# Down-projection of a ConvFFN: one accumulating transfer per result, and six of eight output pairs finished in SBUF

## The chip, the cores and the metric

The kernel runs on one core of one Trainium2 chip. The metric is the device time of one execution in microseconds. Times are the median of several executions; the profile shows one execution.

## What is computed

One inference step of a hybrid layer over T = 592 tokens (16 meta tokens, 512 of a prompt, 8 x 8 samples) with D_MODEL = 2048 and D_FF = 6144, all in float32. Cut to the part that matters:

```python
x = x + jnp.einsum("bte,ed->btd", y_mix, w_o)
xn2 = rmsnorm(x, g_ffn)
up = jnp.einsum("btd,df->btf", xn2, w_up)
gate, val = jnp.split(up, [D_FF], axis=-1)
gate_c, new_fconv = causal_dwconv(gate, st_fconv, conv_f_w)
hid = jax.nn.gelu(gate_c + conv_f_b) * val
x = x + jnp.einsum("btf,fd->btd", hid, w_down)      # the down-projection
...
y = rmsnorm(x, g_final)
```

## The kernel before

Everything is held with features on the 128 partitions and tokens along the free dimension. A float32 factor is split into a high and a low part (`hi`, `lo`; ScalarE copies the rounded high part, VectorE subtracts), and a product takes three matmuls: high by high, high by low, low by high.

**The up- and down-projection use a Strassen-like scheme.** Weights come in pairs of blocks, two by two; tokens are cut into two halves of H2 = 288 columns. Seven products of combined blocks replace eight. `prep` (lines 251 to 284) loads 8 blocks of weights (`raw`, three buffers, issued on SP), forms the combinations on VectorE (one operation of 512 columns, two of 256) and splits seven blocks of each of two units into `wh` and `wl` (four buffers of each). The inputs' combinations are built by `forms` into slots `h0`/`l0` to `h7`/`l7` of the pool `slots`, and one more set in other buffers (`v`, `o`, `st`, `fb`): nine slots for 22 input pairs, so input k lies in slot k mod 9.

**The down-projection runs in three passes** (`s` = 0, 1, 2) over the 22 input pairs k, since only nine are in SBUF at a time. In each pass there is one job ("d", s, p) for each of the eight output pairs p. A job's units are the k from `CUT[p][s]` to `CUT[p][s+1]`: pass 0 takes 4, 5, 6, 7, 8, 8, 9, 9 units for p = 0 to 7, pass 1 takes 9 each, pass 2 takes 9, 8, 7, 6, 5, 5, 4, 4. One unit is 7 products of 3 matmuls with 288 columns. Two units make a group; with an odd number of units a group holds the last unit of one job and the first of the next.

A job's products collect in four PSUM tiles: `s6` (product P6, a single bank), `dq` (P2, Q3), `dp` (P1, R7) and `dr` (P5, R4). There are two buffers for the first kind and three for the others, so the next job's matmuls wait until each is read. When a job ends, `done_d` (lines 471 to 490) turns them into two SBUF tiles of four blocks, `e23` and `e17`, by five ScalarE copies and two VectorE additions, and adds them into two DRAM accumulators per output pair, `xa[p]` (which holds the residual at first) and `xb[p]`, by two transfers on POOL's queue with `accum_op=AD`. `urgent()` raises the priority of these reads.

**The tail** multiplies the last four blocks of `hid` (input pairs 22 and 23, `kh`/`kl`, made by `last_hidden`) without the scheme: for two ranges of tokens (304 and 272 columns) and 16 output blocks f, 12 matmuls each (line 712). `done_t` adds the PSUM result to `xp[f // 2]`, squares it and sums the squares for the final norm. `load_xp` (lines 537 to 541) fetches `xp[p]` from DRAM, first `xa[p]`, then `xb[p]` added onto it. Before the change `xp` of pairs 0 to 2 is asked for when job ("d", 2, 5) ends, the others when all jobs have ended. The tail's weights, eight groups of 8 blocks, are split into `th` and `tl`; they lie in slots 4, 5, 0 and 1 (`TAILW`).

**Order.** The instructions of each engine run in an order that a planner fixes when the kernel is built, from priorities and the durations that it assumes. It may put an instruction ahead of its place in the program: transfers of `kf`, which the code asks for when job ("d", 2, 3) ends, stand in the profile at 2446.80 us, in job ("d", 2, 0). SP issues the loads of weights, POOL all transfers of `sb`, `xa`, `xb`, `xp` and `kf`.

Tiles by name: `raw` weights as loaded, `wh`/`wl` split weights, `fh`/`fl` split inputs, `e` the tiles of `done_d`, `sgl`/`dbl` PSUM, `th`/`tl` split tail weights. Lines 210 and 216 are the helpers through which nearly all VectorE additions and ScalarE copies go, line 552 the matmuls of both projections, line 247 the loads of weights, lines 486, 488 and 490 the accumulations, 540 and 541 the loads of `xp`.

Of the kernel before, what the change touches and what calls it, by code (L numbers as in the profile page):

```python
# [7 lines left out]
F32 = mybir.dt.float32  # L8
F32R = mybir.dt.float32r
AF = mybir.ActivationFunctionType  # L10
ALU = mybir.AluOpType

P = 128
# [4 lines left out]
KD = 16  # L18
NA, NB, NF = 12, 8, 48
# [7 lines left out]
NTF = T - T1  # L27
# [30 lines left out]
NSL = 9  # L58
NWB = 4
NRAW = 3  # L60
TAILW = (4, 5, 0, 1)
NPL = 4
NTL = 4
H1, H2 = NTM // 2, NTF // 2
# [135 lines left out]
def ffn(ctx, tc, xstack, one, dram, x1, rstd, ones, epst, warm, cv, wf, sfc, out, fst):  # L200
# [4 lines left out]
    nc = tc.nc  # L205
    V, A, G = nc.vector, nc.scalar, nc.gpsimd
    M, AD, SU = ALU.mult, ALU.add, ALU.subtract

    def tt(o, a, b, op, e=None):
        return (e or V).tensor_tensor(out=o, in0=a, in1=b, op=op)  # L210
# [4 lines left out]
    def act(o, a, f, **k):  # L215
        A.activation(out=o, in_=a, func=f, **k)  # L216
# [7 lines left out]
    urgent = lambda: tc.high_priority(offset=URGENT)  # L224
# [26 lines left out]
    def prep():  # L251
        q, u = divmod(state["spl"], 2)
        while state["raw"] < min(q + NRAW, len(FG)):
            load()
        t = raws.pop(q) if u else raws[q]
        kind, i, _ = FG[q]
        if kind == "s":
            r = t.rearrange("p (s c) f -> p s (c f)", s=8)
            if u == 0:
                tt(r[:, 4:6], r[:, 2:4], r[:, 0:1].to_broadcast([P, 2, 2 * P]), AD)  # L260
                tt(r[:, 6], r[:, 5], r[:, 2], AD)
                tt(r[:, 7], r[:, 6], r[:, 1], AD)
            src, n = r[:, 1:8, u * P:u * P + P], 7
        else:
            src, n = t[:, 4 * u:4 * u + 4], 4
        if kind == "t":
            if u == 0:
                g = i // 2
                tag = TAILW[g // 2]
                if g % 2 == 0:  # L270
                    for c in "hl":
                        tail[c] = sl.tile([P, 16, P], F32R, tag=f"{c}{tag}", name="t" + c)
                tail[g] = [tail[c][:, 8 * (g % 2):8 * (g % 2) + 8] for c in "hl"]
                hi, lo = tail[g]
                act(hi, t[:, 0:8], AF.Copy)
                tt(lo, t[:, 0:8], hi.bitcast(F32), SU)
            spls[q, u] = None
        else:
            hi = w_p.tile([P, n, P], F32R, tag="wh", name="wh")
            lo = w_p.tile([P, n, P], F32R, tag="wl", name="wl")  # L280
            act(hi, src, AF.Copy)
            tt(lo, src, hi.bitcast(F32), SU)
            spls[q, u] = hi, lo
        state["spl"] += 1
# [10 lines left out]

    xd = [dram.tile([P, 2, NTM], F32, name=f"xd{p}") for p in range(KD // 2)]
    xa = [dram.tile([P, 4, H2], F32, name=f"xa{p}") for p in range(KD // 2)]
    xb = [dram.tile([P, 4, H2], F32, name=f"xb{p}") for p in range(KD // 2)]
    hd = [dram.tile([P, 2, NTF], F32, name=f"hd{m}") for m in range(NF // 2)]
    qa = xq_p.tile([P, 2, NTM], F32, tag="sb", name="qa")  # L300
    qb = xq_p.tile([P, 2, NTM], F32, tag="xt", name="qb")
# [169 lines left out]
    def done_d(s, p, ps):  # L471

        s6, dq, dp, dr = ps
        e6 = rp.tile([P, H2], F32, tag="e6", name="e6")
        e23 = rp.tile([P, 4, H2], F32, tag="e23", name="e23")
        e17 = rp.tile([P, 4, H2], F32, tag="e17", name="e17")
        w = lambda d: d[:, :, 0:H2]
        with urgent():
            act(e6, s6[:, 0:H2], AF.Copy)
            act(e23[:, 0:4:3], w(dq), AF.Copy)  # L480
            act(e23[:, 1], dq[:, 1, 0:H2], AF.Copy, scale=-1.0)
            act(e23[:, 2], dq[:, 0, 0:H2], AF.Copy, scale=-1.0)
            tt(e17[:, 1:3], w(dp), e6.unsqueeze(1).to_broadcast([P, 2, H2]), AD)
            act(e17[:, 0:4:3], w(dp), AF.Copy)
            tt(e17[:, 1:3], w(dr), e17[:, 1:3], AD)
        nc.gpsimd.dma_start(out=xa[p], in_=e23, accum_op=AD)
        if s:
            nc.gpsimd.dma_start(out=xb[p], in_=e17, accum_op=AD)
        else:
            nc.gpsimd.dma_start(out=xb[p], in_=e17)  # L490

    kh, kl = [], []

    def last_hidden():
        ts = []
        for c in range(NTL // 2):
            ts.append(xq_p.tile([P, 2, NTF], F32, tag=("sb", "xt")[c], name="kf"))
            nc.gpsimd.dma_start(out=ts[c], in_=hd[NF // 2 - NTL // 2 + c])
        for c, t in enumerate(ts):
            h = sl.tile([P, 2, NTF], F32R, tag=f"h{6 + c}", name="kh")  # L500
            l = sl.tile([P, 2, NTF], F32R, tag=f"l{6 + c}", name="kl")
            act(h, t, AF.Copy)
            tt(l, t, h.bitcast(F32), SU)
            for j in range(2):
                kh.append(h[:, 1 - j])
                kl.append(l[:, 1 - j])
# [30 lines left out]
    def load_xp(p, pl_, tag):  # L537
        xp[p] = pl_.tile([P, 2, NTF], F32, tag=tag, name="xp")
        w = xp[p].rearrange("p f (h m) -> p (f h) m", h=2)
        nc.gpsimd.dma_start(out=w, in_=xa[p])  # L540
        nc.gpsimd.dma_start(out=w, in_=xb[p], accum_op=AD)

    def products(u, hi, lo, names, ps, H):
        nonlocal mm
# [14 lines left out]
    while FG[q][0] != "t":  # L559
        kind, i, _ = FG[q]  # L560
        halves = weights(q)
        if kind == "p":
            r, k0 = i
            if k0 == 0:
                d = psd()
                ps = [(d[:, 0, 0:H1], d[:, 1, 0:H1])]
                if r == 0:
                    d = psd()
                    ps.append((d[:, 0, 0:H1], d[:, 1, 0:H1]))
                else:  # L570
                    ps.append((pss()[:, 0:H1], pss()[:, 0:H1]))
            for k in range(k0, k0 + 4):
                hi, lo = halves[(k - k0) // 2]
                for j in range(2):
                    o = (k - k0) % 2 * 2 + j
                    rh, rl = ph[k // 2][:, k % 2], pl[k // 2][:, k % 2]
                    for n, (l, x) in enumerate(((hi, rh), (hi, rl), (lo, rh))):
                        for h, (c0, w) in enumerate(HPL):
                            mm = nc.tensor.matmul(ps[j][h], l[:, o], x[:, c0:c0 + w],  # L579
                                                  start=k == 0 and n == 0,  # L580
                                                  stop=k == KD - 1 and n == 2)
            if r == 0 and k0 == 4:
                norm(mm)
            if k0 + 4 == KD:
                (plain_v if r else plain_f)(0, ps)
            if r:
                for kp in (k0 // 2, k0 // 2 + 1):
                    build_x(kp)
        else:
            same = i[0][0] == i[1][0]  # L590
            H = H2 if i[0][0][0] == "d" else H1
            for us in ([i] if same else [[i[0]], [i[1]]]):
                job = us[0][0]
                if job not in pst:
                    pst[job] = (pss(), psd(), psd(), psd())
                    if job == lastc:
                        for k in (0, 1):
                            load_h(k)
                hold = left[job]
                for n in NAMES:  # L600
                    left[job] = hold
                    for u in us:
                        products(u, *halves[i.index(u)], n, pst[job], H)
                        left[job] -= 1
                if left[job] == 0:
                    {"f": done_f, "v": done_v, "d": done_d}[job[0]](*job[1:], pst.pop(job))
                    if job == lastc:
                        nc.gpsimd.dma_start(out=fst.rearrange("p (n c) -> p n c", c=18), in_=fa)
                for u in us:
                    for k in due.get(nunit, ()):  # L610
                        build_h(k)
                    nunit += 1
                if job == ("d", 2, 3) and left[job] == 0:
                    last_hidden()
                if job == ("d", 2, 5) and left[job] == 0:
                    for p, tag in enumerate(("o", "fb", "v")):
                        load_xp(p, rp, tag)
        q += 1

    for p, tag in ((3, "h2"), (4, "l2"), (5, "h3"), (6, "l3")):  # L620
        load_xp(p, sl, tag)

    load_xp(7, rp, "e23")
    sq_a = xq_p.tile([P, 3, 304], F32, tag="sb", name="sq_a")
    sq_b = xq_p.tile([P, 3, 304], F32, tag="xt", name="sq_b")
    sq_c = rp.tile([P, 2, 304], F32, tag="st", name="sq_c")
    rz2 = rp.tile([P, 2, 304], F32, tag="e17", name="rz2")
    SZ = [(sq_a[:, 0], sq_b[:, 0]), (sq_c[:, 0], sq_c[:, 1])]
    SQ = [sq_a[:, 1], sq_b[:, 1], sq_a[:, 2], sq_b[:, 2]]
    later = []  # L630

    def defer(n, fn):
# [624 lines left out]
```

## Time and profile before

| | us |
|---|---|
| median of 3 runs | 2675.44 |
| lowest, highest | 2668.48, 4513.52 |
| profiled execution, its own time | 2674.38 |
| its span in the profile | 2672.6 |
| mean granted clock of TensorE | 0.986 |

| Stretch of the span | us |
|---|---|
| mixer and up-projection | 0 to 2058 |
| down-projection, passes 0 and 1 | 2058 to 2435 |
| pass 2 | 2435 to 2593 |
| tail, first range of tokens | 2593 to 2628 |
| tail, second range | 2628 to 2658 |
| final norm of the second range and its output | 2658 to 2673 |

PE is TensorE's matmuls, PEld its loads of weights, DVE VectorE, ACT ScalarE, POOL GpSimd, SP the engine that issues the loads of weights. In a row of waits, "X <- Y: a, n, m" says that X waited for Y for a us in total, n times, m us at the longest. In a row of the timeline the bracket holds the engine's idle time before the instruction and what ended it. In a group of instructions the numbers behind the bar are busy us and mean ns of one, then idle us before them.

### The profile page before, as it was taken

What the parts mean: (1) busy time and instruction counts of PE and PEld (TensorE: products, weight loads), DVE (VectorE), ACT (ScalarE), POOL (GpSimd) and SP (SyncE); (2) the same over time, 40 slices, a digit from 0 to 9 for tenths busy, and PEclk for the clock granted to TensorE, in tenths of its full rate; (3) what the DMA queues carried; (4) which work ended last, traced back from release to release, by engine and by line L of the source; (5) the groups of instructions that cost most, each with busy time, mean ns of one, the idle gap of its engine ahead of it and who ended that gap; (6) DMA issues with size and microseconds to landing.
All of it is one profiled execution on the core that took longest, in us unless ns stands there. A gap on an engine that the chain in (4) does not pass through costs nothing.

```text
span 2672.6 us, 46445 instructions
## 1 busy us (share of the span) xinstructions
PE 2581.6 (97%) x18974; PEld 2562.4 (96%) x18974; DVE 1960.0 (73%) x2699; ACT 1188.9 (44%) x1760; POOL 503.4 (19%) x636
## 2 busy tenths in 40 slices
PE   8999999999999978999999999999999999999986
PEld 8999999999999977999999999999999999999986
DVE  8663556536636579888888888888889978778655
ACT  6542434334325354454444454545445545435442
POOL 3341323314224530000000000000000100001023
PEclk9999999999999988999999999999999999999989
DMA  5222222222222433333333333333334756656695
GB/s 167 80 88 79 80 80 83 82 82 80 80 80 90 179 128 117 122 104 113 104 106 106 112 103 114 104 114 104 114 104 126 205 147 187 156 145 170 154 233 143
DMA packets 90518, 318.32 MB, mean 119 GB/s; under 512 B 10816, under 2 KB 15424, under 8 KB 90304
## 3 DMA queue, kind: packets, MB, share of 16 engines
q1 hardware_dynamic: 68720, 233.47, 27.9%
q0 software_dynamic: 21152, 81.43, 11.6%
q8 instruction: 148, 2.42, 0.4%
q14 instruction: 66, 0.54, 0.1%
q10 hardware_dynamic: 432, 0.46, 0.1%
HBM read 257.91 MB, written 57.39 MB: 118 GB/s over the span
## 4 chain that ended last, share of the span: by engine, by line
PE 53%; DVE 5%; DMA 4%; issue 1%; ACT 1%; POOL 0%; DVEq 0%; ACTq 0%; POOLq 0%
PE dbl L552 44%; PE sgl L552 7%; DMA raw<-wf 2%; DVE wl L210 2%; PE dbl L579 1%; DMA sb<-hd 1%; DVE fl L210 1%; DMA xp<-xa 1%; DVE raw L210 1%; DVE xt L210 1%; DVE xp L213 1%; DVE sb L213 0%; DMA xp<-xb 0%; PE dbl L712 0%; ACT e L216 0%
## 5 line engine op out<-in xcount | busy, mean ns | idle before, releaser
L552 PE MATMUL dbl<-fh,wh 128*128 128x290 f32 (+1 forms) x3264 | 969.6, 297 | 14.7 <-ACT e L216 10.9
L552 PE MATMUL dbl<-fl,wh 128*128 128x290 f32 (+1 forms) x3264 | 966.8, 296 | 2.2 <-DVE fl L210 2.2
L552 PE MATMUL dbl<-fh,wl 128*128 128x290 f32 (+1 forms) x3264 | 966.4, 296 | 2.1 <-DVE wl L210 2.0
L216 ACT ACTIVATE wh<-raw 128x896 fp32r<-128x896 f32 (+1 forms) x560 | 498.6, 935 | 600.3 <-issue 356.5
L210 DVE TENSOR_TENSOR wl<-raw,wh 128x896 fp32r<-128x896 f32 (+1 forms) x560 | 583.7, 1074 | 106.8 <-ACT wh L216 103.7
L552 PEld LDWEIGHTS dbl<-fh,wh 128*128 128x128 f32 x3264 | 617.7, 189 | 18.8 <-ACT e L216 13.8
L552 PEld LDWEIGHTS dbl<-fl,wh 128*128 128x128 f32 x3264 | 618.5, 190 | 3.3 <-DVE fl L210 3.3
L552 PEld LDWEIGHTS dbl<-fh,wl 128*128 128x128 f32 x3264 | 618.3, 190 | 3.0 <-DVE wl L210 3.0
L210 DVE TENSOR_TENSOR raw<-raw 128x256 f32<-128x256 f32 (+1 forms) x816 | 412.4, 510 | 151.1 <-DMA raw<-wf 141.1
L787 ACT ACTIVATE wh<-raw 128x512 fp32r<-128x512 f32 x277 | 172.5, 628 | 395.6 <-PE ps L1168 343.3
L1168 PE MATMUL ps<-xh,wl 128*128 128x290 f32 (+4 forms) x1536 | 335.6, 299 | 3.7 <-DVE wl L775 3.7
L1168 PE MATMUL ps<-xh,wh 128*128 128x290 f32 (+4 forms) x1536 | 331.3, 297 | 2.9 <-ACT wh L787 2.9
L1168 PE MATMUL ps<-xl,wh 128*128 128x290 f32 (+4 forms) x1536 | 333.8, 299 | 0.0
L775 DVE TENSOR_TENSOR wl<-raw,wh 128x512 fp32r<-128x512 f32 x192 | 152.9, 802 | 193.0 <-ACT wh L787 192.6
L1168 PEld LDWEIGHTS ps<-xh,wl 128*128 128x128 f32 x1536 | 256.8, 190 | 4.2 <-DVE wl L775 4.2
L1168 PEld LDWEIGHTS ps<-xh,wh 128*128 128x128 f32 x1536 | 256.7, 190 | 3.8 <-ACT wh L787 3.1
L1168 PEld LDWEIGHTS ps<-xl,wh 128*128 128x128 f32 x1536 | 254.9, 189 | 0.0
L775 POOL TENSOR_TENSOR wl<-raw,wh 128x512 fp32r<-128x512 f32 x86 | 117.9, 1371 | 312.5 <-ACT wh L787 302.5
L552 PE MATMUL sgl<-fh,wl 128*128 128x290 f32 (+1 forms) x544 | 164.8, 303 | 10.0 <-DVE wl L210 9.9
L552 PE MATMUL sgl<-fh,wh 128*128 128x290 f32 (+1 forms) x544 | 162.3, 298 | 3.3 <-ACT wh L216 2.5
L552 PE MATMUL sgl<-fl,wh 128*128 128x290 f32 (+1 forms) x544 | 162.2, 298 | 2.6 <-DVE fl L210 2.6
L1168 PE MATMUL ps<-kh,wl 128*128 128x290 f32 x640 | 138.5, 297 | 0.0
(222 smaller groups left out, 3219.5 us busy)
## 6 DMA issues: line engine op xcount, KB each, us to landing
raw<-wf SPq DMA_DIRECT2D x288, 512.0 KB, 3.6
raw<-w SPq DMA_DIRECT2D x135, 512.0 KB, 3.6
hd<-v POOLq DMA_DIRECT2D x48, 288.0 KB, 2.8
xa<-e POOLq DMA_DIRECT2D x24, 576.0 KB, 7.4
xb<-e POOLq DMA_DIRECT2D x24, 576.0 KB, 7.1
sb<-hd POOLq DMA_DIRECT2D x22, 576.0 KB, 4.4
x<-x SPq DMA_DIRECT2D x16, 296.0 KB, 5.3
xd<-x POOLq DMA_DIRECT2D x16, 290.0 KB, 2.6
```

Of the source, the lines that this page charges most:

```text
L210: return (e or V).tensor_tensor(out=o, in0=a, in1=b, op=op)
L213: V.scalar_tensor_tensor(out=o, in0=a, scalar=s, in1=b, op0=op0, op1=op1)
L216: A.activation(out=o, in_=a, func=f, **k)
L552: mm = nc.tensor.matmul(o, l[a], r[z], start=left[job] == total[job] and n == 0, stop=left[job] == 1 and n == 2)
L579: mm = nc.tensor.matmul(ps[j][h], l[:, o], x[:, c0:c0 + w], start=k == 0 and n == 0, stop=k == KD - 1 and n == 2)
L775: return (e or V).tensor_tensor(out=o, in0=a, in1=b, op=op)
L787: A.activation(out=o, in_=a, func=f, **k)
L1168: mm = nc.tensor.matmul(ps[:, b, 0:n], l, r[:, c0:c0 + n], start=(first and m == 0), stop=(last and m == 2))
```

## The change

`done_d` is rewritten. In passes 0 and 1, and for output pairs 0 and 1 of pass 2, it forms all four blocks in one tile `e` (buffers `e17` and `e23` in turn) with four ScalarE copies and four VectorE additions, and adds that tile into `xa[p]` by one accumulating transfer; `xb` is gone. For output pairs 2 to 7 of pass 2 it adds the PSUM tiles to `xp[p]` in SBUF, by seven VectorE operations, with no ScalarE copy and no transfer.

For that `xp[p]` of pairs 2 to 7 is loaded during pass 2 into slots 4, 5 and 6, when jobs 0, 1 and 2 end; pairs 0 and 1 are loaded into `e17` and `e23` when job 3 ends. Each load is one transfer. `kf`, the input of `last_hidden`, is loaded when job 0 ends, and split when job 5 ends, into other buffers. The tail's weights move: group 0 to the buffers of `kf`, groups 1 to 6 to slots 1, 2 and 3, group 7 to `l7`. The squares of the final norm move to slot 0.

```diff
         if kind == "t":
             if u == 0:
                 g = i // 2
-                tag = TAILW[g // 2]
-                if g % 2 == 0:
-                    for c in "hl":
-                        tail[c] = sl.tile([P, 16, P], F32R, tag=f"{c}{tag}", name="t" + c)
-                tail[g] = [tail[c][:, 8 * (g % 2):8 * (g % 2) + 8] for c in "hl"]
+                if g == 0:
+                    tail[g] = [xq_p.tile([P, 8, P], F32R, tag=c, name="t" + c) for c in ("sb", "xt")]
+                elif g == 7:
+                    t7 = sl.tile([P, 16, P], F32R, tag="l7", name="t7")
+                    tail[g] = [t7[:, 0:8], t7[:, 8:16]]
+                else:
+                    j, o = divmod(g + 1, 2)
+                    if o == 0:
+                        tail["h"], tail["l"] = (sl.tile([P, 16, P], F32R, tag=f"{c}{j}", name="t" + c)
+                                                for c in "hl")
+                    tail[g] = [tail[c][:, 8 * o:8 * o + 8] for c in "hl"]
...
     def done_d(s, p, ps):
 
         s6, dq, dp, dr = ps
-        e6 = rp.tile([P, H2], F32, tag="e6", name="e6")
-        e23 = rp.tile([P, 4, H2], F32, tag="e23", name="e23")
-        e17 = rp.tile([P, 4, H2], F32, tag="e17", name="e17")
         w = lambda d: d[:, :, 0:H2]
+        if s < 2 or p < 2:
+            e6 = rp.tile([P, H2], F32, tag="e6", name="e6")
+            e = rp.tile([P, 4, H2], F32, tag=("e17", "e23")[p % 2], name="e")
+            on, off = e[:, 0:4:3], e[:, 1:3]
+            with urgent():
+                act(e6, s6[:, 0:H2], AF.Copy)
+                act(on, w(dq), AF.Copy)
+                act(e[:, 1], dq[:, 1, 0:H2], AF.Copy, scale=-1.0)
+                act(e[:, 2], dq[:, 0, 0:H2], AF.Copy, scale=-1.0)
+                tt(off, w(dp), off, AD)
+                tt(on, w(dp), on, AD)
+                tt(off, w(dr), off, AD)
+                tt(off, off, e6.unsqueeze(1).to_broadcast([P, 2, H2]), AD)
+            nc.gpsimd.dma_start(out=xa[p], in_=e, accum_op=AD)
+            return
+        t = xp[p].rearrange("p f (h m) -> p (f h) m", h=2)
+        on, off = t[:, 0:4:3], t[:, 1:3]
         with urgent():
-            act(e6, s6[:, 0:H2], AF.Copy)
-            act(e23[:, 0:4:3], w(dq), AF.Copy)
-            act(e23[:, 1], dq[:, 1, 0:H2], AF.Copy, scale=-1.0)
-            act(e23[:, 2], dq[:, 0, 0:H2], AF.Copy, scale=-1.0)
-            tt(e17[:, 1:3], w(dp), e6.unsqueeze(1).to_broadcast([P, 2, H2]), AD)
-            act(e17[:, 0:4:3], w(dp), AF.Copy)
-            tt(e17[:, 1:3], w(dr), e17[:, 1:3], AD)
-        nc.gpsimd.dma_start(out=xa[p], in_=e23, accum_op=AD)
-        if s:
-            nc.gpsimd.dma_start(out=xb[p], in_=e17, accum_op=AD)
-        else:
-            nc.gpsimd.dma_start(out=xb[p], in_=e17)
+            tt(off, s6[:, 0:H2].unsqueeze(1).to_broadcast([P, 2, H2]), off, AD)
+            tt(on, w(dq), on, AD)
+            tt(t[:, 1], t[:, 1], dq[:, 1, 0:H2], SU)
+            tt(t[:, 2], t[:, 2], dq[:, 0, 0:H2], SU)
+            tt(on, w(dp), on, AD)
+            tt(off, w(dp), off, AD)
+            tt(off, w(dr), off, AD)
...
+    def load_last():
+        for c in range(NTL // 2):
+            kfs.append(xq_p.tile([P, 2, NTF], F32, tag=("sb", "xt")[c], name="kf"))
+            nc.gpsimd.dma_start(out=kfs[c], in_=hd[NF // 2 - NTL // 2 + c])
+
     def last_hidden():
...
-            h = sl.tile([P, 2, NTF], F32R, tag=f"h{6 + c}", name="kh")
-            l = sl.tile([P, 2, NTF], F32R, tag=f"l{6 + c}", name="kl")
+            h = (sl, rp)[c].tile([P, 2, NTF], F32R, tag=("h7", "fb")[c], name="kh")
+            l = rp.tile([P, 2, NTF], F32R, tag=("o", "v")[c], name="kl")
...
         nc.gpsimd.dma_start(out=w, in_=xa[p])
-        nc.gpsimd.dma_start(out=w, in_=xb[p], accum_op=AD)
...
-                if job == ("d", 2, 3) and left[job] == 0:
-                    last_hidden()
-                if job == ("d", 2, 5) and left[job] == 0:
-                    for p, tag in enumerate(("o", "fb", "v")):
-                        load_xp(p, rp, tag)
+                if job[0] == "d" and job[1] == 2 and left[job] == 0:
+                    n = job[2]
+                    if n == 0:
+                        load_last()
+                    for p, tag in {0: ((2, "h4"), (3, "l4")), 1: ((4, "h5"), (5, "l5")),
+                                   2: ((6, "h6"), (7, "l6"))}.get(n, ()):
+                        load_xp(p, sl, tag)
+                    if n == 3:
+                        for p, tag in ((0, "e17"), (1, "e23")):
+                            load_xp(p, rp, tag)
+                    if n == 5:
+                        last_hidden()
...
-    for p, tag in ((3, "h2"), (4, "l2"), (5, "h3"), (6, "l3")):
-        load_xp(p, sl, tag)
-
-    load_xp(7, rp, "e23")
-    sq_a = xq_p.tile([P, 3, 304], F32, tag="sb", name="sq_a")
-    sq_b = xq_p.tile([P, 3, 304], F32, tag="xt", name="sq_b")
...
+    sq_a = sl.tile([P, 6, 304], F32, tag="h0", name="sq_a")
+    sq_b = sl.tile([P, 4, 304], F32, tag="l0", name="sq_b")
...
```

More of the change, by code (lines that the diff above doesn't have):

```diff
@@ L60 @@
 NRAW = 3
-TAILW = (4, 5, 0, 1)
 NPL = 4
@@ L297, in ffn @@
     xa = [dram.tile([P, 4, H2], F32, name=f"xa{p}") for p in range(KD // 2)]
-    xb = [dram.tile([P, 4, H2], F32, name=f"xb{p}") for p in range(KD // 2)]
     hd = [dram.tile([P, 2, NTF], F32, name=f"hd{m}") for m in range(NF // 2)]
@@ L486, in done_d @@
-        nc.gpsimd.dma_start(out=xa[p], in_=e23, accum_op=AD)
-        if s:
-            nc.gpsimd.dma_start(out=xb[p], in_=e17, accum_op=AD)
-        else:
-            nc.gpsimd.dma_start(out=xb[p], in_=e17)
-    kh, kl = [], []
-    def last_hidden():
[L495 to L499, printed above, removed]
-            h = sl.tile([P, 2, NTF], F32R, tag=f"h{6 + c}", name="kh")
-            l = sl.tile([P, 2, NTF], F32R, tag=f"l{6 + c}", name="kl")
+        if s < 2 or p < 2:
[13 more added lines that the diff above has]
+            return
@@ new lines, in done_d @@
+        t = xp[p].rearrange("p f (h m) -> p (f h) m", h=2)
+        on, off = t[:, 0:4:3], t[:, 1:3]
+        with urgent():
+            tt(off, s6[:, 0:H2].unsqueeze(1).to_broadcast([P, 2, H2]), off, AD)
[5 more added lines that the diff above has]
+            tt(off, w(dr), off, AD)
+    kh, kl = [], []
+    kfs = []
+    def load_last():
+        for c in range(NTL // 2):
+            kfs.append(xq_p.tile([P, 2, NTF], F32, tag=("sb", "xt")[c], name="kf"))
+            nc.gpsimd.dma_start(out=kfs[c], in_=hd[NF // 2 - NTL // 2 + c])
@@ L502, in last_hidden @@
+    def last_hidden():
+        for c, t in enumerate(kfs):
+            h = (sl, rp)[c].tile([P, 2, NTF], F32R, tag=("h7", "fb")[c], name="kh")
+            l = rp.tile([P, 2, NTF], F32R, tag=("o", "v")[c], name="kl")
             act(h, t, AF.Copy)
@@ L612, in ffn @@
                     nunit += 1
-                if job == ("d", 2, 3) and left[job] == 0:
-                    last_hidden()
-                if job == ("d", 2, 5) and left[job] == 0:
-                    for p, tag in enumerate(("o", "fb", "v")):
-                        load_xp(p, rp, tag)
-        q += 1
-    for p, tag in ((3, "h2"), (4, "l2"), (5, "h3"), (6, "l3")):
-        load_xp(p, sl, tag)
-    load_xp(7, rp, "e23")
-    sq_a = xq_p.tile([P, 3, 304], F32, tag="sb", name="sq_a")
-    sq_b = xq_p.tile([P, 3, 304], F32, tag="xt", name="sq_b")
[L626 to L629, printed above, removed]
+                if job[0] == "d" and job[1] == 2 and left[job] == 0:
[10 more added lines that the diff above has]
+                        last_hidden()
+        q += 1
+    sq_a = sl.tile([P, 6, 304], F32, tag="h0", name="sq_a")
+    sq_b = sl.tile([P, 4, 304], F32, tag="l0", name="sq_b")
+    SZ = [(sq_a[:, 0], sq_a[:, 1]), (sq_b[:, 0], sq_b[:, 1])]
+    SQ = [sq_a[:, 2 + n] for n in range(4)]
+    rz2 = sq_b[:, 2:4]
     later = []
```

## The prediction, made before the changed kernel was run

> **What bounds the kernel now.** I read the page first, then the stretches of the down-projection one by one, then what TensorE (PE) waits for in its end, then the instructions around single waits.
>
> ```profile
> span 2672.6 us, 46445 instructions
> PE 2581.6 (97%) x18974; PEld 2562.4 (96%) x18974; DVE 1960.0 (73%) x2699; ACT 1188.9 (44%) x1760; POOL 503.4 (19%) x636
> ```
>
> PE is busy for 97% of the span, and the change leaves every matmul as it is. So it can only win PE's waits in the down-projection and behind it, or add new ones. The next view has one row per stretch: length, busy time of PE, PEld, DVE, ACT and POOL with the number of instructions in brackets, granted clock, DMA share, GB/s.
>
> ```profile
> 2000.00:2020.00 20.00, 20.00 (x152) 20.00 (x151) 17.29 (x26) 8.73 (x15) 0.05 (x1) 1.00 0.34 100
> 2058.00:2436.00 378.00, 365.04 (x2697) 359.40 (x2695) 310.56 (x450) 182.05 (x242) 34.16 (x49) 1.00 0.60 165
> 2151.00:2224.00 73.00, 72.72 (x550) 72.50 (x549) 55.70 (x78) 33.62 (x44) 4.50 (x7) 1.00 0.56 159
> 2224.00:2252.00 28.00, 25.72 (x187) 24.64 (x186) 26.61 (x41) 15.02 (x19) 3.08 (x5) 1.00 0.66 200
> 2436.00:2467.00 31.00, 27.82 (x190) 26.90 (x191) 25.87 (x39) 15.41 (x22) 3.45 (x5) 0.94 0.64 181
> 2467.00:2556.90 89.90, 87.00 (x650) 86.05 (x649) 59.06 (x85) 39.58 (x57) 11.63 (x15) 1.00 0.69 174
> 2556.90:2574.10 17.20, 14.20 (x86) 13.71 (x85) 10.52 (x14) 4.42 (x6) 3.22 (x4) 0.80 1.05 234
> 2574.10:2592.70 18.60, 11.54 (x86) 11.07 (x84) 9.35 (x9) 9.98 (x16) 1.72 (x2) 0.93 0.77 207
> 2592.70:2627.70 35.00, 29.75 (x192) 28.76 (x193) 13.90 (x26) 13.67 (x25) 13.19 (x17) 0.94 0.96 232
> ```
>
> The undisturbed row, 2151 to 2224, gives the unit: 73.0 us for 550 matmuls, 0.1327 us each. In pass 3 pair p takes 9, 8, 7, 6, 5, 5, 4, 4 units of 21 matmuls, and the stretches are cut where the pairs begin. Against the unit, pair 0 (2436 to 2467) needs 189 x 0.1327 = 25.1 us and loses 5.9; pairs 1 to 5 need 651 x 0.1327 = 86.4 and lose 3.5; pair 6 needs 84 x 0.1327 = 11.1 and loses 6.1; pair 7 loses 7.5; the first half of the tail (192 matmuls with 304 columns, so 0.140 us each, 26.9 us) loses 8.1. From pair 1 on that is **25.2 us**. The first two passes need 2688 x 0.1327 = 357 us of 378 and lose 21.
>
> What PE waits for, from pass 3 to the middle of the tail (total, times, longest):
>
> ```profile
> PE sgl L552 <- DVE wl L210: 5.8, 6, 3.0
> PE dbl L552 <- ACT e L216: 5.5, 4, 2.1
> PE dbl L712 <- DVE xp L210: 5.2, 4, 2.3
> PE dbl L712 <- ACT e L216: 5.0, 1, 5.0
> ```
>
> There are three causes: weights split late (`wl`), the PSUM of the pair before read late (`e`), and the tail's additions late (`xp`). Behind all three stand transfers. First the additions, with VectorE's (DVE) wait in the tail and the transfers between 2540 and 2640 (KB, median us to landing); the last row is a load of weights in the quiet up-projection:
>
> ```profile
> DVE xp L210 <- DMA xp<-xb: 15.8, 5, 4.6
> ...
> raw<-wf SPq DMA_DIRECT2D x11, 512.0 KB, 7.1
> xp<-xa POOLq DMA_DIRECT2D x8, 576.0 KB, 8.5
> xp<-xb POOLq DMA_DIRECT2D x8, 576.0 KB, 7.6
> ...
> raw<-wf SPq DMA_DIRECT2D x25, 512.0 KB, 3.5
> ```
>
> Loads of weights land in 7.1 us instead of 3.5, because 16 `xp` transfers and the last accumulations share the DMA engines (share 0.77 to 1.05 in the last three stretches). Now the end of a job, pair 3 of pass 2 ahead of its neighbour:
>
> ```profile
> 2303.43 0.69 DVE L210 TENSOR_TENSOR raw<-raw 128x512 f32<-128x512 f32 x1 [1.66 <-DMA raw<-wf]
> ...
> 2304.04 2.09 DVE L210 TENSOR_TENSOR wl<-raw,wh 128x896 fp32r<-128x896 f32 x2
> ...
> 2306.04 0.75 DVE L210 TENSOR_TENSOR e<-dbl,e 128x576 f32<-128x576 f32 x1
> ...
> 2306.83 0.65 ACT L216 ACTIVATE e<-dbl 128x576 f32<-128x576 f32 x1 [1.88 <-DVE e L210]
> ```
>
> The last of these is what PE's waits for `ACT e` stand at: ScalarE (ACT) had itself waited 1.88 us for DVE, which had stood 1.66 us at late weights and then had two splits ahead. The wait belongs to DVE and DMA.
>
> **The change part by part.** DVE's instructions in pairs 1 to 7 of pass 3 by form, and the nearest form with 288 columns out of PSUM:
>
> ```profile
> L210 DVE TENSOR_TENSOR wl<-raw,wh 128x896 fp32r<-128x896 f32 x36 | 37.8, 1085 | 3.2 <-ACT wh L216 3.2
> L210 DVE TENSOR_TENSOR raw<-raw 128x256 f32<-128x256 f32 x34 | 14.3, 421 | 0.7
> L210 DVE TENSOR_TENSOR raw<-raw 128x512 f32<-128x512 f32 x17 | 11.7, 691 | 32.8 <-DMA raw<-wf 32.8
> L210 DVE TENSOR_TENSOR e<-dbl,e 128x576 f32<-128x576 f32 x14 | 10.5, 751 | 0.4
> L210 DVE TENSOR_TENSOR tl<-raw,th 128x1024 fp32r<-128x1024 f32 x5 | 6.0, 1223 | 9.7 <-ACT th L216 9.6
> L210 DVE TENSOR_TENSOR kl<-kf,kh 128x1152 fp32r<-128x1152 f32 x2 | 2.7, 1351 | 0.0
> ...
> L210 DVE TENSOR_TENSOR v<-dbl,v 128x290 f32<-128x290 f32 x2 | 0.8, 445 | 0.0
> ```
>
> *Passes 1 and 2, and pairs 0 and 1 of pass 3 (18 jobs).* Each loses one accumulation of 576 KB and one ACT copy (0.65 us), and gains two DVE operations of 576 columns: 2 x 0.75 = 1.5 us. The second PSUM pair (`dp`) was freed by that ACT copy, 0.65 us, right behind DVE's first operation; now DVE's second one frees it, 0.75 us later. So where a job ends on half a group nothing new stands in the way of the next, as long as `dq`, which the same ACT copies read, is ready as before. The added DVE time has cover in most places: DVE is idle for 378 - 310.6 = 67 us of the first two passes. It has none while new inputs are built (26.6 busy of 28 us in 2224 to 2252, 25.9 of 31 in 2436 to 2467, and the first job). Three such places at 1.5 us cost 4 to 5 us. Against this, one of two accumulations per job leaves the DMA engines, so weights land earlier than now, and DVE's stand at them ahead of the PSUM reads (1.66 us in the rows above) shrinks. Bounds: +27 us (18 x 1.5, no cover) to -10 us (half of the 21 lost); I take **0**, the value nearest the row of 2151 to 2224, where DVE has 17 us to spare in 73 and PE does not wait.
>
> *Pairs 2 to 7: the moved loads.* `xp` is loaded into slots that pass 3 has finished with. Pair 2's load can begin when pair 0's first matmuls are done, some 3 us behind 2436, and is needed at 2510, where pair 2 ends: over 60 us for 8.5. Eight loads, now one transfer each, go between 2440 and 2530, in place of accumulations that leave; I cost them at nothing, and if that cover is gone they show as later weights in pairs 0 to 3. POOL, which issues them, has nothing else urgent queued there.
>
> *Pairs 2 to 7: the new chain.* No ACT copies and no transfers; DVE does five operations of 576 (0.751) and two of 288 (0.445): 5 x 0.751 + 2 x 0.445 = 4.65 us per pair, where it did 1.5. That is 3.15 x 6 = 18.9 us more. Queued behind them on DVE are the weight splits, and PE waits for those. In pairs 5, 6 and 7 PE needs 13 units x 21 x 0.1327 = 36.2 us. DVE needs per group of two units 2 x 1.085 + 0.691 + 2 x 0.421 = 3.70, so 24.1 for 6.5 groups, 13.9 for three chains, 2.7 for `kl` and 2.4 for two `tl`: 43.1, less about 0.08 for each of its 57 operations (two `wl` in a row take 2.09, not 2.17), 38.5 us. DVE is short by 2 us, and pair 7's chain runs partly into the tail. In pairs 2 to 4 (18 units, 50 us) it needs 33 + 14 = 47, which just fits; in the up-projection DVE is busy 17.29 of 20 us and PE has no wait at all. So I leave 5 us of loss in pairs 1 to 7 (bounds 0, as in the up-projection, and 15: a pair of splits, 2.09 us, ahead of each of six chains, and 2.5 behind it).
>
> *The tail.* No `xp` transfer is left in it but for pairs 0 and 1, loaded after pair 3. The 16 transfers that followed the last accumulation are gone, so the additions wait for PE alone, and the weights' loads for little. Tail weights for all but the first and last group now go to slots that pair 7 still reads. Split and rest of group 1 (1.06 on ACT, 1.22 on DVE) fit behind pair 7's first group, 5.6 us before its end; groups 3 to 6 begin at its end and are needed 10 us into the tail. I leave 1 us of loss of the 8.1.
>
> Clock: the row of 2556.9 to 2574.1 has 0.80 behind a wait of 3.00 us, the tail's first half 0.94 behind 5.04, while the longest of the waits for `ACT e` on L552, 2.1 us, left no such row:
>
> ```profile
> 2560.35 0.61 PE L552 MATMUL sgl<-fh,wl 128*128 128x288 f32 x1 [3.00 <-DVE wl L210]
> ...
> 2592.75 0.62 PE L712 MATMUL dbl<-kh,th 128*128 128x304 f32 x1 [5.04 <-ACT e L216]
> ```
>
> These slow matmuls are inside the losses above and go with the waits; no wait of 3 us is in what I leave. The Trainium skill, "TensorE: Matmul & The Clock Gate", Part 1, has the clock halve after an idle window of about 3.4 us; the trace has it after 3.00 us, so a DVE chain that holds PE that long would cost about the wait again.
>
> A rule that speaks against the change: the Trainium skill, "DMA: Bandwidth & Descriptors", section on the anatomy of a DMA on the GpSimd path, gives 2.0 us plus bytes over 436 GB/s, by estimate 3.4 us for 576 KB. By it the tail's old loads would hide, and the gain there would not exist. The rows above (7.6 and 8.5 us, and 15.8 us of waiting) disagree.
>
> **Sum.** 25.2 lost from pair 1 on becomes 5 + 1: 19.2 us gained, the rest 0. The profiled execution took 2674.4 us (span 2672.6), so 2655.2; the median of three, 2675.44, is 1.1 higher: **2656 us**.
>
> **The rivals.**
> - *DVE takes the place of the waits in pass 3 (0.16).* Each chain begins behind two splits, PE waits about 2 us at each of six ends and once long enough for the clock: 15 us lost instead of 6, gain 10: 2666. For it: 38.5 us of work in 36.2; against it: 46 us of idle DVE in pairs 1 to 7 (125.7 - 78.9), 32.8 of them at late weights.
> - *The relief reaches the first two passes as well (0.17).* Weights land in 3.5 us again, DVE is on time, 8 of the 21 us go: 2648. For it: the chain at 2303; against it: the builds, where DVE is full.
> - *Slower: DVE becomes the bound of the whole down-projection (0.08).* Added DVE work is 18 x 1.5 + 18.9 = 46 us. If all of it delays PE, 25 gained and 46 lost: 2696. It decides from 25/46, 55% of the added work on PE's path. Against it: 67 us of idle DVE in the first two passes.
> - *The tail gains nothing (0.02).* Its 8.1 us stay, if what holds it is not the `xp` transfers but something behind them, such as the late tail weights: gain 12, 2663. Against it: 15.8 us of DVE's waits there name `xp`, none names weights for PE. The rule of the skill on transfers, above, would point this way.
> - *The change does not do what it says (0.02).* The planner of the instruction order puts the `xp` loads late, additions wait as now: 2676. The 60 us of room speak against it.
>
> **How the numbers follow.** My forecast, 2656 (2649 to 2663), has 0.55. The range takes in both neighbours and no gain: 2644 to 2677; above it lies most of the slower case. Faster by over 2% (about what a measurement of this kernel can tell from no change) means below 2622: a gain of 53 us, where all the loss of the down-projection and the tail's first half comes to 52 (25.2 + 5.9 + 21): 0.01. Slower by over 2%, above 2729, needs more than twice the slower case: 0.02. Within: 0.97.
>
> **What would show it.** Right: first half of the tail at 27 to 29 us, pairs 6 and 7 at 11 to 14 each, clock 1.00 there, no `PE dbl L712 <- DVE xp` waits of over 1 us, loads of weights under 4 us after 2540, first two passes within 5 us of 378. Wrong: waits of PE for `wl` or for a DVE `xp` chain at the ends of pairs 4 to 7, or a longer pass 1.

## Result and profile after

The changed kernel takes 2656.93 us (median of 4 runs), the kernel before 2673.95 in its 4: ratio 0.9942 [0.9929, 0.9954]. That is 17.0 us less, no change by the bound of 2%, against 19.2 and 2656 in the prediction. One of the four runs before took 4513.52 us; the ratio leaves it out, and without it the difference is 15.5 us. The profiled execution of the changed kernel took 2659.82 us, 2.9 above the median. Its page:

```profile
span 2657.5 us, 46406 instructions
...
PE 2583.6 (97%) x18974; PEld 2565.9 (97%) x18974; DVE 1999.1 (75%) x2765; ACT 1166.6 (44%) x1712; POOL 473.3 (18%) x598
...
q0 software_dynamic: 15680, 59.01, 7.6%
```

The matmuls are the same 18974, DVE is busy 39 us longer, ACT 22 us less. The total hides shifts in opposite directions. They show in the stretches of the changed kernel, cut where its jobs begin: passes 0 and 1, pairs 0, 1 and 2 of the third pass, pairs 3 to 5, pairs 6 and 7, first half of the tail (columns as in the prediction's rows):

```profile
2063.30:2439.70 376.40, 365.18 (x2691) 359.85 (x2690) 328.16 (x480) 173.94 (x226) 24.11 (x35) 0.99 0.51 142
2439.70:2467.70 28.00, 26.31 (x191) 25.22 (x190) 24.24 (x37) 13.67 (x20) 3.19 (x6) 1.00 0.68 221
2467.70:2496.60 28.90, 24.78 (x170) 23.88 (x169) 19.22 (x27) 8.64 (x13) 2.51 (x4) 0.94 0.53 155
2496.60:2520.40 23.80, 21.72 (x150) 21.17 (x148) 15.94 (x25) 5.92 (x8) 2.56 (x4) 0.93 0.68 188
2520.40:2565.00 44.60, 44.60 (x338) 44.57 (x337) 38.95 (x61) 16.30 (x18) 0.00 (x0) 1.00 0.29 85
2565.00:2576.20 11.20, 11.20 (x87) 11.20 (x86) 11.09 (x18) 4.65 (x5) 0.00 (x0) 1.00 0.34 102
2576.20:2587.30 11.10, 11.10 (x85) 11.10 (x85) 10.89 (x16) 4.12 (x5) 0.00 (x0) 1.00 0.50 163
2587.30:2614.10 26.80, 26.80 (x194) 26.80 (x193) 18.76 (x31) 15.88 (x28) 5.19 (x5) 1.00 0.20 65
```

From pair 3 to the middle of the tail PE is busy in every microsecond. Pairs 1 and 2, 168 and 147 matmuls at 0.1327 us, need 22.3 and 19.5 us and take 28.9 and 23.8.

The span is 15.1 us shorter: third pass 157.35 us against 147.6 now (9.75 gained), first half of the tail 35.0 against 26.8 (8.2), passes 0 and 1 376.75 against 376.4 (0.35), the rest 44.9 against 43.4 (1.5). From that go 4.66 us: the down-projection begins at 2063.3 instead of 2058.7, though none of its work has been edited up to there.

PE's waits in the changed kernel, third pass to the middle of the tail's second half:

```profile
PE sgl L567 <- DVE wl L209: 5.5, 6, 2.0
PE dbl L567 <- DVE e L209: 2.3, 2, 1.8
```

The waits for `ACT e` are gone, and in this stretch those for the tail's `xp` (one of 0.9 us comes later, at 2634.57); all that are left lie in pairs 0 to 2. The weights' loads, with the transfers of the changed kernel between 2540 and 2640:

```profile
raw<-wf SPq DMA_DIRECT2D x13, 512.0 KB, 3.6
y<-xp SPq DMA_DIRECT2D x8, 304.0 KB, 2.3
```

They land in 3.6 us where they took 7.1: no transfer into `xa` or `xp` is in that stretch any more.

Where the new loss in pairs 1 and 2 comes from, in the changed kernel's timelines of POOL, SP, DVE and PE:

```profile
2471.78 0.37 PE L567 MATMUL dbl<-fh,wh 128*128 128x288 f32 x1 [1.76 <-DVE e L209]
...
2473.87 0.55 POOL L556 DMA_DIRECT2D xp<-xa  x1 [19.79 <-PE dbl L567]
2474.61 0.88 POOL L492 DMA_DIRECT2D xa<-e  x1 [0.19 <-ACT wh L215]
2475.18 0.85 POOL L556 DMA_DIRECT2D xp<-xa  x1
...
2475.67 0.33 SPq L246 DMA_DIRECT2D raw<-wf  x1
...
2484.59 0.69 DVE L209 TENSOR_TENSOR raw<-raw 128x512 f32<-128x512 f32 x1 [7.09 <-DMA raw<-wf]
2485.20 2.08 DVE L209 TENSOR_TENSOR wl<-raw,wh 128x896 fp32r<-128x896 f32 x2
...
2486.34 0.40 PE L567 MATMUL sgl<-fh,wl 128*128 128x288 f32 x1 [1.99 <-DVE wl L209]
...
2487.75 0.44 PE L567 MATMUL dbl<-fh,wh 128*128 128x288 f32 x1
2487.99 0.44 PE L567 MATMUL dbl<-fl,wh 128*128 128x288 f32 x1
...
2490.39 0.44 PE L567 MATMUL dbl<-fh,wl 128*128 128x288 f32 x1
2490.63 0.34 PE L567 MATMUL dbl<-fh,wh 128*128 128x288 f32 x1
2490.80 0.29 PE L567 MATMUL dbl<-fl,wh 128*128 128x288 f32 x1
...
2500.50 0.54 POOL L556 DMA_DIRECT2D xp<-xa  x1 [15.17 <-PE dbl L567]
2501.24 0.91 POOL L492 DMA_DIRECT2D xa<-e  x1 [0.20 <-ACT wh L215]
2501.84 0.87 POOL L556 DMA_DIRECT2D xp<-xa  x1
...
2511.11 0.69 DVE L209 TENSOR_TENSOR raw<-raw 128x512 f32<-128x512 f32 x1 [6.98 <-DMA raw<-wf]
...
2512.85 0.41 PE L567 MATMUL sgl<-fh,wl 128*128 128x288 f32 x1 [1.75 <-DVE wl L209]
...
2514.63 0.44 PE L567 MATMUL dbl<-fl,wh 128*128 128x288 f32 x1
...
2517.75 0.42 PE L567 MATMUL dbl<-fh,wl 128*128 128x288 f32 x1
```

Read it downwards. The first row is a loss of its own, ahead of the transfers: PE waits 1.76 us for DVE, until the merged tile's additions have read the PSUM of pair 0. Then POOL waits 19.79 us for the last matmul that reads slot 5, in pair 1's first unit, then issues two loads of `xp` and, between them, the accumulation of pair 0, three transfers of 576 KB within 1.3 us. The weights that SP asks for at 2475.67 reach DVE at 2484.59, 8.9 us later. DVE stands 7.09 us, PE 1.99, and twelve of the matmuls that follow start 0.24 us apart instead of 0.13. Pair 2 repeats it from 2500.50 on: the same three transfers, 6.98 us of DVE's time, and a wait of PE of 1.75 us.

### The profile page after: what moved, and what is told of

Same layout as the page of the kernel before. It is cut to its first block, busy times and chain, and to the rows that moved or that the text cites. A ratio compares the mean times of both kernels' runs of the same rounds, so it can differ in the third digit from the quotient of the medians.

```text
span 2657.5 us, 46406 instructions
## 1 busy us (share of the span) xinstructions
PE 2583.6 (97%) x18974; PEld 2565.9 (97%) x18974; DVE 1999.1 (75%) x2765; ACT 1166.6 (44%) x1712; POOL 473.3 (18%) x598
```

## Experiments

All were run beside the kernel before; the letters of the theories are those of the texts on record. "Loss" is the time of a stretch over its matmuls at 0.1327 us (0.140 in the tail), worked out from each profile. The last column is the start of the down-projection.

| kernel | median us | ratio to before [95%] | loss pairs 0 / 1 / 2 | 3-5 / 6 / 7 / tail | start |
|---|---|---|---|---|---|
| before | 2673.95 | | 6.2 / 0.3 / 1.8 | 1.9 / 6.0 / 7.5 / 8.1 | 2058.7 |
| changed | 2656.93 | 0.9942 [0.9929, 0.9954] | 3.0 / 6.6 / 4.3 | 0 / 0 / 0 / -0.1 | 2063.3 |
| e1 | 2653.95 | 0.9927 [0.9914, 0.9939] | 2.5 / 1.4 / 1.1 | 1.6 / 4.6 / 0.2 / 1.4 | 2058.6 |
| e2 | 2659.07 | 0.9950 [0.9937, 0.9962] | 8.8 / 1.7 / 6.6 | 0.1 / 0 / 0 / -0.1 | 2062.5 |
| e3 | 2647.70 | 0.9905 [0.9892, 0.9919] | 2.4 / 1.4 / 1.5 | 0.1 / 0 / 0 / -0.1 | 2061.6 |
| e4 | 2657.08 | 0.9944 [0.9930, 0.9957] | 2.5 / 6.1 / 3.5 | 0.4 / 1.1 / 1.4 / -0.1 | 2061.5 |
| e5 | 2650.52 | 0.9915 [0.9901, 0.9928] | 6.9 / 0 / 0.1 | 0.3 / 0 / 0 / -0.1 | 2062.1 |
| e6 | 2657.70 | 0.9938 [0.9926, 0.9951] | 3.0 / 5.8 / 2.8 | 0 / 0 / 0 / -0.1 | 2062.3 |
| e7 | 2660.11 | 0.9949 [0.9936, 0.9961] | 2.7 / 1.2 / 0.8 | 1.3 / 4.8 / 0.5 / 2.7 | 2064.4 |
| e8 | 2649.42 | 0.9909 [0.9895, 0.9922] | 4.8 / 0.1 / 0 | 0 / 0 / 0 / -0.1 | 2062.2 |
| e9 | 2645.76 | 0.9893 [0.9880, 0.9907] | 5.4 / 0 / 0 | 0 / 0 / 0 / 0.3 | 2058.3 |
| e10 | 2656.61 | 0.9935 [0.9923, 0.9948] | 3.0 / 7.2 / 2.6 | 0.1 / 0 / 0 / -0.1 | 2061.6 |
| e11 | 2655.68 | 0.9931 [0.9918, 0.9943] | 3.1 / 0.7 / 1.0 | 1.8 / 4.6 / 0.4 / 2.7 | 2059.0 |
| e12 | 2648.93 | 0.9904 [0.9889, 0.9920] | 5.1 / 0.1 / 0.1 | 0.1 / 0 / 0 / -0.1 | 2062.4 |

e1 to e4 shared one chip and its runs of before, e5 to e8 another, e9 to e12 a third.

### e1, e11: one transfer per result alone

The kernel before, with the merged `done_d` for all 24 jobs; loads of `xp` in their old places, one transfer each.

```diff
-        nc.gpsimd.dma_start(out=xa[p], in_=e23, accum_op=AD)
...
+            tt(off, off, e6.unsqueeze(1).to_broadcast([P, 2, H2]), AD)
+        nc.gpsimd.dma_start(out=xa[p], in_=e, accum_op=AD)
...
-        nc.gpsimd.dma_start(out=w, in_=xb[p], accum_op=AD)
```

> The kernel before with only the first part of the change: all 24 jobs form one tile by four ScalarE copies and four VectorE additions and send one accumulating transfer; the loads of xp (now one transfer each), the tail's weights and kf stay where they were. Theory A (the gain is at the end and comes from transfers that no longer crowd it): half of the end's transfers are left, so about half of the 25 us lost from pair 1 on remain; gain 8 to 14 us, 2660 to 2666, ratio 0.995 to 0.997, with the first two passes within 3 us of before. Theory B (halving the transfers is all that matters, finishing in SBUF adds nothing): the whole gain of the change, 2657, ratio 0.994. Theory C (the two added VectorE operations cost in every job): first two passes 10 us or more longer, no gain.

Measured 2653.95 us, 0.9927 [0.9914, 0.9939]: halving the transfers alone gives the whole gain. e11 is the same kernel again, beside the changed kernel again (e10):

> The changed kernel itself, unaltered, on the same chip as the next two, so that the three can be compared: 2656 to 2658 (ratio 0.994), with 10 to 11 us lost in pairs 1 and 2 of pass 2 and none from pair 3 on.

> The one-transfer variant again: if finishing six pairs in SBUF as the change does it gives nothing over one transfer per job (theory B), it is 2 to 5 us faster than the changed kernel on the same chip, 2652 to 2655; if the first comparison was chance, they are equal.

On one chip they give 0.9935 [0.9923, 0.9948] and 0.9931 [0.9918, 0.9943]: no difference. Pair 7 and the tail, 15.6 us of loss before, keep 1.6 (e1) and 3.1 (e11) without one pair completed in SBUF. What e1 keeps is pair 6 (row of its windows):

```profile
2552.50:2568.20 15.70, 13.19 (x86) 12.73 (x85) 12.86 (x18) 5.90 (x10) 0.87 (x1) 0.89 0.47 124
```

4.6 us, with clock 0.89. From pair 0 to the tail e11 loses 14.3 us and e10 12.8, so completing six pairs in SBUF is worth 1.5 us there, and e10 gives 2.6 back by its later start, which e6 to e9 put down to the layout of the buffers.

### e2: six pairs in SBUF alone

The changed kernel with two tiles, two accumulators and two transfers in the jobs that still accumulate, and two transfers per load of `xp`.

```diff
+            nc.gpsimd.dma_start(out=xa[p], in_=e23, accum_op=AD)
+            if s:
+                nc.gpsimd.dma_start(out=xb[p], in_=e17, accum_op=AD)
...
+        nc.gpsimd.dma_start(out=w, in_=xb[p], accum_op=AD)
```

> The changed kernel with the first part undone: passes 0 and 1 and pairs 0 and 1 of pass 2 send two tiles to two accumulators as before, and each load of xp is two transfers in series; pairs 2 to 7 are finished in SBUF. Theory A (the end gains because it has no transfers; the moved loads cost 9 us in pairs 1 and 2 of pass 2 because weights land late there): the end gains the same 22 us, pairs 0 to 2 lose 15 to 25 us because 16 instead of 8 moved transfers lie there; 2660 to 2668. Theory B (the end gains from the halving): the gain is gone, 2670 or more with waits back in the tail. Theory C (pairs 1 and 2 lose through VectorE's added operations): they lose less than the 10.7 us of the changed kernel, 2650 to 2655.

2659.07 us, and the pass shows the price of twice the transfers, loads and accumulations: pairs 0 and 2 of e2 have a DMA share of 0.82 and 0.93 and lose 8.8 and 6.6 us.

```profile
2439.90:2473.80 33.90, 28.67 (x191) 27.37 (x191) 25.42 (x38) 15.09 (x21) 6.24 (x9) 0.90 0.82 235
2497.70:2523.80 26.10, 22.01 (x149) 21.08 (x148) 17.12 (x26) 6.61 (x9) 6.56 (x9) 0.93 0.93 224
```

From pair 3 on nothing is lost. So each half of the change clears most of the end by itself, and the two gains do not add.

### e3: the moved loads taken away

`xp` of pairs 2 to 7 is set to zero instead of loaded.

```diff
-        nc.gpsimd.dma_start(out=w, in_=xa[p])
+        if p > 1:
+            G.memset(xp[p], 0.0)
+        else:
+            nc.gpsimd.dma_start(out=w, in_=xa[p])
```

> The changed kernel with the six moved loads left out: xp of pairs 2 to 7 is set to zero on GpSimd instead, so the residual and the sums of the first two passes are missing from these outputs. Theory A (the moved loads delay weights in pairs 1 and 2): the loss there falls from 10.7 us to 1 to 3, all else as in the changed kernel; 2647 to 2650, ratio 0.990 to 0.991. Theory C (VectorE's added work in pairs 0 and 1 is the cause): pairs 1 and 2 lose as before, 2656 to 2658.

2647.70 us, 9 less than the changed kernel. Pairs 1 and 2 of e3:

```profile
2464.10:2487.80 23.70, 22.49 (x170) 22.29 (x169) 16.59 (x25) 8.64 (x13) 3.58 (x4) 1.00 0.49 139
2487.80:2508.80 21.00, 19.71 (x149) 19.50 (x148) 16.85 (x26) 5.91 (x8) 3.56 (x4) 1.00 0.55 154
```

They lose 2.9 us instead of 10.9, at clock 1.00. The moved loads cost 8 us there, and that is nearly all of the 9. What is left is above all PE's wait for DVE's `e`, 1.2 and 1.3 us some 3 us into the two pairs. e1, with the same merged tile, has it in pair 1 too (1.14 us); the kernel before and e2, without that tile, have none in pair 1.

### e4: two more operations in each chain

```diff
+            tt(off, w(dr), off, AD)
+            tt(off, off, w(dr), SU)
```

> The changed kernel with two more VectorE operations of 576 columns out of PSUM in each chain of pairs 2 to 7 (dr subtracted and added once more, 1.3 us per pair, 8 us in all). In the changed kernel VectorE is busy 10.99 of 11.1 us in pair 6 and 10.99 of 11.2 in pair 7, with no wait of TensorE. Theory D (VectorE is at its limit there, every further operation delays TensorE in pairs 5 to 7): 3 to 6 us longer than the changed kernel, 2660 to 2663, with TensorE waiting for splits or for xp at the ends of pairs 5 to 7. Theory E (its fullness is work done ahead of need, room is left): within 1 us of the changed kernel, 2656 to 2658.

The time stays (2657.08 us), but not because there is room. Pairs 6 and 7 of e4:

```profile
2559.80:2572.10 12.30, 11.77 (x87) 11.30 (x86) 12.13 (x20) 4.66 (x5) 0.00 (x0) 1.00 0.28 87
2572.10:2584.60 12.50, 11.67 (x85) 11.14 (x85) 12.46 (x19) 3.63 (x4) 0.00 (x0) 1.00 0.38 126
```

DVE is busy 12.13 of 12.30 and 12.46 of 12.50 us, and PE, which lost nothing here, loses 1.1 and 1.4 us. Twelve operations of 0.75 us, 9 us of work, cost 2.9 us with pairs 3 to 5: the changed kernel stands just below the point where DVE becomes the bound. By the median alone the two theories cannot be told apart; the starts of the down-projection and pairs 1 and 2 vary by more.

### e5, e12: all eight pairs in SBUF

```diff
-        if s < 2 or p < 2:
+        if s < 2:
...
+                if job == ("d", 1, 7) and left[job] == 0:
+                    for p, tag in ((0, "e17"), (1, "e23")):
+                        load_xp(p, rp, tag)
...
-                    if n == 3:
-                        for p, tag in ((0, "e17"), (1, "e23")):
-                            load_xp(p, rp, tag)
```

> The changed kernel with pairs 0 and 1 finished in SBUF as well: xp of 0 and 1 is loaded into e17 and e23 at the end of pass 1, and pass 2 has no accumulating transfer at all (two accumulations fewer in pairs 1 and 2; still eight loads). Theory A (pairs 1 and 2 lose 10.9 us because two loads and an accumulation begin together there and weights land late): without the accumulations the loss is about halved, 4 to 6 us faster than the changed kernel, 2651 to 2653. Theory H (any two loads at the end of a pair delay the weights as much): pairs 1 and 2 lose 9 or more, 2655 to 2657; or VectorE's longer chain in pairs 0 and 1 adds waits of its own.

> All eight pairs in SBUF again, beside the two: 2649 to 2652, 5 to 8 us faster than the changed kernel and 2 to 5 faster than the one-transfer variant.

2650.52 and 2648.93 us, 6 to 8 below the changed kernel. Pairs 1 and 2 of e5:

```profile
2469.60:2491.90 22.30, 22.30 (x170) 22.26 (x169) 17.94 (x28) 7.29 (x8) 1.07 (x2) 1.00 0.47 148
2491.90:2511.50 19.60, 19.60 (x150) 19.57 (x149) 16.41 (x26) 5.80 (x7) 1.07 (x2) 1.00 0.46 143
```

The loads of `xp` are there, two at a time, and nothing is lost; the accumulations of pairs 0 and 1 are gone, with the copies and additions that formed their tiles. With e3 (accumulations, no loads) that shows that neither delays the weights by enough alone: it is their coming together. The slowest load of weights in pair 1 says how much is enough. Where it lands 5.8 us (e3) or 6.5 us (e5) after it is asked for, PE does not wait for it; at 7.6 us (e2) PE waits 0.48, at 7.9 (e4) 0.75, at 8.9 (the changed kernel) 1.99. So pair 1 hides, by estimate from these runs, some 7 us of a load, and PE stands for what is above that. Pair 0, which must now have its `xp` early and is completed on DVE, loses 2 to 4 us more than in the changed kernel; which of the two does it was not tried.

### e6, e7, e8, e9: where the up-projection's 3 to 5 us went

Nothing in the up-projection was edited, and PE has no wait in it, yet its matmuls come more slowly in the changed kernel. One row each, of before and of the changed kernel:

```profile
1600.00:1700.00 100.00, 100.00 (x752) 100.00 (x751) 84.12 (x123) 47.61 (x77) 6.86 (x12) 1.00 0.35 108
```

```profile
1600.00:1700.00 100.00, 100.00 (x749) 100.00 (x748) 83.37 (x122) 47.17 (x73) 6.83 (x12) 1.00 0.35 108
```

That is 133.9 ns from matmul to matmul instead of 133.5. From its 200th matmul on, the up-projection takes 1007.97 us instead of 1004.94, 3.0 us more; in e10, the same program, it takes 1007.97 too. The other 1.6 us of the changed profile's 4.66 lie in the first 50 us of the up-projection, at a lower granted clock (before, then changed):

```profile
1007.00:1056.00 49.00, 38.23 (x224) 34.10 (x223) 47.44 (x69) 21.29 (x28) 5.61 (x10) 0.86 0.32 105
1007.00:1056.00 49.00, 39.12 (x208) 34.84 (x208) 45.69 (x68) 19.57 (x24) 5.91 (x10) 0.79 0.33 104
```

e10 does not have them (its 200th matmul comes at 1053.6, that of before at 1053.7), so they belong to that one execution; the 3.0 us are what needs a cause. The edits change the sizes of slots, and so the addresses of the buffers behind them. (The addresses here are worked out from the sizes of the tiles; no trace shows them.) e6 puts the changed kernel's `kh` into a slot 64 bytes longer, which puts the weights' buffers (`raw`, `wh`, `wl`) back to 64 bytes past a multiple of 128, as the program before has them; e8 does the same to e5; e7 lengthens the slot `h6` of e1 by 64 bytes, and nothing else; e9 gives all slots of e5 one size, 8192 bytes, so that all begin 64 bytes past a multiple of 128, as most do before.

```diff
# e6, e8
-            h = (sl, rp)[c].tile([P, 2, NTF], F32R, tag=("h7", "fb")[c], name="kh")
+                h = sl.tile([P, 16, P], F32R, tag="h7", name="kh").rearrange("p a b -> p (a b)")
...
# e7
+            h = sl.tile([P, 16, P] if c == 0 else [P, 9, P], F32R, tag=f"h{6 + c}", name="kh").rearrange("p a b -> p (a b)")
...
# e9
+        big = lambda t, n: sl.tile([P, 2, 1024], F32R, tag=t, name=n)[:, :, 0:NTM]
```

> The changed kernel with one buffer (slot h7, for kh) made 72 elements... that is 64 bytes a partition longer, so that the raw and split weights behind it lie again at addresses of 64 modulo 128 bytes, as in the kernel before; in the changed kernel they lie at 0 modulo 128. Theory F (the place of the operands in SBUF sets the matmuls' rate: 749 per 100 us in the up-projection of the changed kernel and its variants, 752 before and in the one-transfer variant): the up-projection is back at 752, the down-projection begins at 2058.6 and not 2061.5 to 2063.3; 3 to 4 us faster, 2652 to 2654. Theory G (run to run, or another order of instructions): no change, 2656 to 2658.

> The one-transfer variant (which took 2654 us, its weights at 64 modulo 128) with slot h6 made 64 bytes longer, so that the weights lie at 0 modulo 128. Theory F: it loses what the changed kernel lost, 749 matmuls per 100 us in the up-projection and 3 to 4 us in all: 2657 to 2658. Theory G: 2653 to 2655.

> All eight pairs finished in SBUF, and the 64 bytes as well. If both theories A and F hold, their gains add: 2647 to 2650, faster than the changed kernel by 7 to 10 us and than the one-transfer variant (2654) by 4 to 7. If only one holds, 2651 to 2654.

> All eight pairs finished in SBUF, with every one of the 16 slots made 8192 bytes a partition long, so that all slots and the weights behind them lie at 64 modulo 128 bytes. Theory F2 (the rate of the matmuls goes by the slots' places, and 64 modulo 128 is the good one, as most slots have it in the kernel before): 752 matmuls per 100 us in the up-projection, the down-projection begins at 2058.6, and the kernel is 3 us faster than all-eight without it, 2646 to 2648. If the rate goes by something else in the layout: 747 to 751, 2649 to 2655.

e6 (749 matmuls, 2657.70 us) and e8 (2649.42) changed nothing, so the place of the weights' buffers alone is not it. e7 and e9:

```profile
1600.00:1700.00 100.00, 100.00 (x747) 100.00 (x747) 83.03 (x122) 47.15 (x73) 6.93 (x12) 1.00 0.35 108
```

```profile
1600.00:1700.00 100.00, 100.00 (x752) 100.00 (x751) 84.13 (x123) 47.72 (x77) 6.83 (x12) 1.00 0.34 108
```

64 bytes in one slot cost e1 five matmuls in 100 us (134.3 ns from one to the next) and 4 to 6 us of time (2653.95 us, 2655.68 in e11, to 2660.11; its down-projection starts 5.8 us later than e1's). The kernel before, e1 and e11 have 133.5 ns on different chips, the changed kernel, e10, e2 to e5 and e12 133.9, so chance is out. Slots of one size give the 752 back, and e9 starts the down-projection at 2058.3. It is the fastest version: 2645.76 us, 0.9893 [0.9880, 0.9907], against the changed kernel's 0.9935 on the same chip. That the layout sets this rate is shown; which address decides is open.

## Why the prediction was right

The number came out right, the sum behind it only in part, and that the median lies 1 us from the forecast is in good part luck: errors of opposite sign met. From pair 1 to the tail 10.8 us of loss are left instead of 6, but in the wrong place: 10.9 in pairs 1 and 2, whose new transfers had been costed at nothing, and none of the 6. Outside that stretch 5.0 us gained (pair 0, the first passes, the end) stand against 4.7 lost by the later start; neither was in the sum. The profiled execution, for which the sum gave 2655.2, took 2659.8.

- *Passes 0 and 1, net 0*: 0.35 us gained (11.2 and 8.5 us lost in the two, where it was 9.3 and 10.7). The added DVE work, 328 busy against 310, found its cover; fewer transfers bought nothing here. That "nothing new stands in the way of the next" job after half a group did not hold at the end of pair 0 in the third pass: there PE waits 1.76 us for DVE's additions; the kernel before has no wait there.
- *Pair 0, in the same net 0*: lost 3.0 instead of 6.2, a gain of 3.2 not forecast.
- *The moved loads, "I cost them at nothing"*: **this step failed.** Pairs 1 and 2 lost 10.9 us, where they lost 2.1; without the moved loads (e3) they lose 2.9, so the term is 8 us. The reason given was 60 us of room for transfers of 8.5; room was there. What was not counted is the moment at which they can begin: one matmul frees the slots of two loads, just when the accumulation of the pair before is issued too. The sign named for it ("later weights in pairs 0 to 3") is what shows, and e3 and e5 bear it out.
- *The new chain, 5 us left*: 0 in pairs 3 to 7. The term was too large. DVE was as full as counted (11.09 busy of 11.2 and 10.89 of 11.1 us in pairs 6 and 7, chain operations of 0.75 and 0.445 us), but the deficit of 2 us supposed that DVE begins level with PE. It enters them ahead: from pair 4 to pair 7 it never waits for weights, which land in 3.6 us, but 1.8 us for PE. e4 shows how little is left.
- *The tail, 1 us left*: 0; the first half takes 26.8 us, a little under the 27 to 29 expected.
- *Clock*: 1.00 from pair 3 to the tail, as forecast. That no wait below 3 us slows it was wrong. In pairs 1 and 2 the waits of 1.99 us and of 1.75 us are followed by 12 and 14 matmuls 0.24 us apart, 1.3 and 1.5 us more, and clocks of 0.94 and 0.93; the wait of 1.76 us at 2471.78 is followed by none, so the length of one wait does not decide it. The Trainium skill, "TensorE: Matmul & The Clock Gate", Part 1, has the clock halve after an idle window of about 3.4 us; these rows do not agree with that as a lower limit.
- *Not in the sum*: the later start, 2.9 (e10) to 4.7 us, of which 3.0 by layout, and 1.5 us gained behind the tail's first half.

Summed, in the profiled executions: pairs 3 to 7 and the tail gave 23.6 us, pair 0 3.2, the passes before and the end behind 1.9, pairs 1 and 2 took 8.8 and the later start 4.7: 15.2 of the span's 15.1.

Of the rivals, DVE as the bound fell for this kernel, in the third pass and so in the whole down-projection too, but e4 reaches it. The relief did not reach passes 0 and 1. That the tail gains nothing fell: with its transfers gone, so are its waits. The change does what it says: no transfer into `xp` is left beside the tail. What the prediction did not see at all is that the second half of the change adds next to nothing to the first (e10 and e11), since it pays for the end with pairs 1 and 2 and with a layout that costs 3.0 us; it pays only once the last two accumulations go as well (e12, 7 us below e11).

## What to carry to other kernels

For a moved transfer, ask not only how long it has but what frees its buffer and what else is issued at that moment: three transfers of 576 KB released together held a load of weights for 8.9 us, where in the quiet up-projection it takes 3.5. Test each half of a change by itself: here either clears most of the end, and their gains do not add. When a stage that nobody edited moves by a few tenths of a per cent without a wait, compare the count of matmuls per 100 us, and look at buffer sizes before looking for a cause in the schedule.

## What the runs showed of the hardware

The rate of matmuls on split float32 operands depends on where the buffers lie in SBUF: 752, 749 or 747 in 100 us, all with PE busy throughout and clock 1.00, from slots that differ by 64 bytes (e1 and e7). In the same kernel 14 matmuls ran at half the rate (0.24 us apart instead of 0.13) after a wait of 1.75 us, and none after one of 1.76 us.
